# SwiGLU's first product by seven block products for eight in half of its chunks (one core of a Trainium2 chip)

## The chip, the cores and the metric

The kernel runs on one core of one Trainium2 chip. The metric is the device time of one execution in microseconds (us); three runs of the kernel before gave a median of 2055.57 us. Engines are named as in the profile: PE is TensorE (matmuls), PEld its weight loads, DVE is VectorE, ACT is ScalarE, POOL is GpSimd, SP is SyncE, which issues the loads.

## What is computed

One layer of a hybrid decoder on 256 tokens of width 2048 in float32: a mixer of three branches, a cross-attention, and the part that the change touches, a gated feed-forward of hidden width 5632:

```python
def swiglu(h, w13, w2):
    a, b = jnp.split(h @ w13, 2, axis=-1)
    return (jax.nn.silu(a.astype(jnp.float32)) * b.astype(jnp.float32)).astype(h.dtype) @ w2
...
        x = x + swiglu(rmsnorm(x, norm_ffn[i]), ffn_w13[i], ffn_w2[i])
    return rmsnorm(x, norm_final)
```

## The kernel before

**Blocks, chunks, halves.** Every product with a weight matrix is made in blocks of 512 output columns. A block's weights come as chunks of 512 rows (a tile `raw`, 128 x 4 x 512, 1 MB, loaded through SP's queue); a chunk is worked off in two halves of two 128-row tiles. The 256 tokens are two tiles of 128, so a block's result is 2 x 512 columns in PSUM, a tile `mm` of two banks; two such tiles exist, and four more banks of PSUM (`tp`) for everything else.

**Three products for one.** To keep float32's accuracy each operand is split in a high part, which TensorE's fp32r takes exactly, and the low rest. For a half chunk ScalarE makes the high part `wh` with one cast of 128x1024 (L161) and VectorE the low part `wl` by one subtraction of 128x1024 (L162). Then come, for two row tiles and two token tiles, three matmuls of 512 columns: high by high (L178), high by low (L179), low by high (L180): 12 for a half chunk. Activations are transposed and split the same way and kept (an `Act` with `hi` and `lo`).

**What sets the order.** The program is a list of halves and calls that is written out in order (`emit_half`); a half's split is emitted up to `LA = 3` halves ahead of its products, `wh` and `wl` have four buffers each and `raw` five. Evictions, transposes and the like are tasks that move one step after each half (`pump`). A scheduler then orders each engine's instructions by a simulated time; each engine works through its own list in order.

**SwiGLU.** The first product has 11 pairs of blocks: block i gives a, block 11 + i gives b, each of four chunks, 16 halves and 192 matmuls of 512 columns a pair. ScalarE makes silu of a, times the tokens' norm (L913), VectorE multiplies by b, times the norm again (L921); the result is transposed on TensorE (L264, two groups of four) and split (L268, L269) as `hT[i]`. The activations `x2T` carry the norm's gain but not the norm itself, which is multiplied in behind the product. After six pairs the second product (`w_2`) of those six chunks is added to the residual (L932), after the other five the rest.

## Time and profile before

| | |
|---|---|
| time, median of 3 runs | 2055.57 us (2055.42 to 2056.17) |
| span of the profiled execution (its time isn't listed apart from the span) | 2054.3 us |
| TensorE busy | 2042.2 us, 99% |
| VectorE busy | 1194.7 us, 58% |
| ScalarE busy | 959.8 us, 47% |
| matmuls of 128x512 in one pair of blocks | 192 |
| one pair of blocks | 44.45 us |

A row gives start and length in us, engine, line, operation, output and inputs (names without buffer numbers), and in brackets how long the engine had been idle and who released it. A matmul's row is longer than the distance to the next one, since matmuls overlap. A wait is put down to what came last.

### The profile page before, as it was taken

The page shows a single profiled execution, that of the slowest core. Times are in us where ns is not written, and L with a number is a line of the kernel's source. Part 1 is how long each engine was busy: PE and PEld are TensorE (multiplying, and loading weights), DVE is VectorE, ACT ScalarE, POOL GpSimd, SP SyncE. Part 2 cuts the span into 40 slices and gives each one's busy share as a digit, 9 for nine tenths or more (in the row PEclk, how much of TensorE's full clock was granted, in tenths as well). Part 3 has the DMA queues.
Part 4 walks back from the last instruction along what each step waited for, and adds up shares of the span by engine and source line. Part 5 has one row for each costly group of instructions (what it writes and reads, how often), then busy time and mean ns, then how long its engine had stood idle before and what let it go on. Part 6 is the DMA issues. An engine that isn't in the chain of part 4 may idle for free.

```text
span 2054.3 us, 23424 instructions
## 1 busy us (share of the span) xinstructions
PE 2042.2 (99%) x9369; PEld 1689.4 (82%) x9369; DVE 1194.7 (58%) x1505; ACT 959.8 (47%) x1190; POOL 20.3 (1%) x32
## 2 busy tenths in 40 slices
PE   9999999999999999999999999999999999999998
PEld 6888888888888888888888888888888888888886
DVE  6995699776654557444455555544455444455445
ACT  7444444558444455444445554444444334444443
POOL 0000000000000000000000000000000000000000
PEclk9999999999999999999999999999999999999999
DMA  9555444444555655655555444555555556555552
GB/s 374 185 188 202 174 175 174 166 164 163 186 212 196 220 200 215 227 203 185 200 186 182 151 149 158 184 185 188 196 189 184 189 200 207 195 192 185 185 199 88
DMA packets 57277, 390.33 MB, mean 190 GB/s; under 512 B 6480, under 2 KB 6736, under 8 KB 11984
## 3 DMA queue, kind: packets, MB, share of 16 engines
q1 hardware_dynamic: 54720, 380.44, 51.6%
q0 software_dynamic: 2304, 8.39, 1.1%
q8 instruction: 73, 1.20, 0.2%
q14 instruction: 36, 0.29, 0.0%
q10 hardware_dynamic: 144, 0.01, 0.0%
HBM read 386.72 MB, written 2.10 MB: 189 GB/s over the span
## 4 chain that ended last, share of the span: by engine, by line
PE 99%; DMA 0%; issue 0%; DVE 0%; SPq 0%; ACTq 0%; ACT 0%; POOLq 0%; POOL 0%
PE mm L178 31%; PE mm L179 31%; PE mm L180 31%; PE tp L264 1%; PE tp L178 1%; PE tp L179 1%; PE tp L180 1%; PE tp L283 0%; PE tp L832 0%; PE tp L831 0%; PE tp L830 0%; DMA raw<-in_w_in 0%; PE tp L622 0%; PE tp L558 0%; PE tp L620 0%
## 5 line engine op out<-in xcount | busy, mean ns | idle before, releaser
L162 DVE TENSOR_TENSOR wl<-raw,wh 128x1024 fp32r<-128x1024 f32 (+1 forms) x705 | 860.8, 1222 | 780.8 <-ACT wh L161 780.3
L161 ACT CAST wh<-raw 128x1024 fp32r<-128x1024 f32 (+1 forms) x705 | 740.8, 1052 | 956.2 <-PE mm L180 909.8
L178 PE MATMUL mm<-wh,s 128*128 128x512 f32 x2752 | 1078.4, 392 | 1.6 <-ACT wh L161 1.6
L179 PE MATMUL mm<-wl,s 128*128 128x512 f32 x2752 | 1075.3, 391 | 1.2 <-DVE wl L162 1.2
L180 PE MATMUL mm<-wh,s 128*128 128x512 f32 x2752 | 1073.7, 390 | 0.0
L178 PEld LDWEIGHTS mm<-wh,s 128*128 128x128 f32 x2752 | 516.8, 188 | 109.4 <-ACT wh L161 3.3
L180 PEld LDWEIGHTS mm<-wh,s 128*128 128x128 f32 x2752 | 516.7, 188 | 107.8
L179 PEld LDWEIGHTS mm<-wl,s 128*128 128x128 f32 x2752 | 517.0, 188 | 106.9 <-DVE wl L162 2.4
L433 DVE SCALAR_TENSOR_TENSOR s<-s,prm_t,s 128x227 f32<-128x227 f32 (+29 forms) x240 | 98.2, 464 | 0.0
L264 PE MATMUL tp<-cst_t,s 128*128 128x128 f32 x280 | 42.7, 272 | 0.0
L264 PEld LDWEIGHTS tp<-cst_t,s 128*128 128x128 f32 x280 | 34.5, 140 | 7.9
L269 DVE TENSOR_TENSOR s<-tp,s 128x512 fp32r<-128x512 f32 x46 | 31.1, 682 | 0.0
L251 ACT ACTIVATE s<-tp,prm_t 128x256 fp32r<-128x256 f32 x40 | 18.6, 472 | 19.1 <-DVE s L252 16.8
L268 ACT CAST s<-tp 128x512 fp32r<-128x512 f32 x46 | 26.4, 582 | 0.5 <-PE tp L264 0.5
L178 PE MATMUL tp<-wh,s 128*128 128x512 f32 x64 | 24.9, 389 | 0.0
L179 PE MATMUL tp<-wl,s 128*128 128x512 f32 x64 | 24.9, 389 | 0.0
L180 PE MATMUL tp<-wh,s 128*128 128x512 f32 x64 | 24.9, 389 | 0.0
L252 DVE SCALAR_TENSOR_TENSOR s<-tp,prm_t,s 128x256 fp32r<-128x256 f32 x40 | 19.0, 480 | 9.1 <-ACT s L251 9.1
L913 ACT ACTIVATE s<-mm,rs 128x512 f32<-128x512 f32 x22 | 13.9, 686 | 16.7 <-PE mm L180 16.7
L694 ACT ACTIVATE s<-mm,rsx 128x512 f32<-128x512 f32 x24 | 15.2, 685 | 12.5 <-PE mm L180 12.4
L296 ACT ACTIVATE s<-s 128x512 f32<-128x512 f32 x32 | 19.9, 624 | 1.4 <-DVE s L758 1.4
L921 DVE SCALAR_TENSOR_TENSOR s<-mm,rs,s 128x512 f32<-128x512 f32 x22 | 15.5, 747 | 4.6 <-PE mm L180 4.6
(172 smaller groups left out, 682.2 us busy)
## 6 DMA issues: line engine op xcount, KB each, us to landing
raw<-in_w SPq DMA_DIRECT2D x132, 1024.0 KB, 4.8
raw<-in_w_in SPq DMA_DIRECT2D x117, 1024.0 KB, 4.8
raw<-in_w_kv SPq DMA_DIRECT2D x32, 1024.0 KB, 4.8
raw<-in_w_br SPq DMA_DIRECT2D x24, 1024.0 KB, 4.8
raw<-in_w_out SPq DMA_DIRECT2D x16, 1024.0 KB, 4.8
raw<-in_w_q SPq DMA_DIRECT2D x16, 1024.0 KB, 4.9
raw<-in_w_o SPq DMA_DIRECT2D x16, 1024.0 KB, 4.8
raw<-in_w_in SPq DMA_DIRECT2D x5, 512.0 KB, 9.3
```

The source lines that it names most:

```text
L161: sc.copy(hi[:, sl, :], rv[:, sl, :])
L162: ve.tensor_tensor(out=lo[:, sl, :], in0=rv[:, sl, :], in1=hi[:, sl, :].bitcast(F32), op=ALU.subtract)
L178: nc.tensor.matmul(ps[t], ah, hi[:, k, :], start=j["start"] and k == 0, stop=False)
L179: nc.tensor.matmul(ps[t], ah, lo[:, k, :], start=False, stop=False)
L180: nc.tensor.matmul(ps[t], al, hi[:, k, :], start=False, stop=stop and k == 1)
L251: sc.activation(a.hi[:, k, :], src, AF.Identity, scale=g)
L252: ve.scalar_tensor_tensor(out=a.lo[:, k, :], in0=src, scalar=g, in1=a.hi[:, k, :].bitcast(F32), op0=ALU.mult, op1=ALU.subtract)
L264: nc.tensor.transpose(tp[:, k, t * P:(t + 1) * P], src(2 * pr + k, t), ident)
L268: sc.copy(a.hi[:, sl, :], tp)
L269: ve.tensor_tensor(out=a.lo[:, sl, :], in0=tp, in1=a.hi[:, sl, :].bitcast(F32), op=ALU.subtract)
L296: sc.activation(junk[:, t, :], tl[:, t, :], AF.Square, accum_out=dst[:, t:t + 1])
L433: ve.scalar_tensor_tensor(out=o[:, s:], in0=uT[:, k, :T - s], scalar=pc("cw", c * CW + CW - 1 - s), in1=o[:, s:], op0=ALU.mult, op1=ALU.add)
```

## The change

In ten of the eleven pairs (all but the first) two of the four chunks (`SC = (0, 1)`) are taken for both blocks at once. The activation chunk is seen as 2 x 2 blocks (token half by row half), the two weight chunks as 2 x 2 blocks (row half by block): a product of 2 x 2 blocks, by seven block products where eight would be the plain way. `quad_jobs` makes the seven units p1 to p7, each of six matmuls; three use the weights as they are (p1, p2, p3), four use differences of weight blocks, made in place in `raw` (L312) and split like the rest. On the activations' side the sums are made once, in `normalised` (`shi`, `slo`); it also multiplies the norm into the activations, so that silu and the product with the gate need it no more. p1, p5, p6 and p7 gather in four `tp` banks over both chunks, p2 and p4 go straight into the first block's `mm`, p3 into the second's. `leave` combines the four banks into two tiles (L372 on ScalarE, L373 to L376 on VectorE); the other two chunks follow by halves as before, and `done` adds the combined tile to each block (L384) before silu and the product. While the two chunks run, tasks that need a `tp` bank are held back (`lock`).

With it come: the first pair taken chunk by chunk in turn (`pair_n`), so that `normalised` can begin; three groups of the second product instead of two (after pairs 3, 7 and 10, counted from 0); `LA = 4`; six buffers for `wh` and `wl`, four for `raw`, 27 for `s4`, which now also holds cross-attention's score tiles (`SX`).

```diff
-LA = 3
+LA = 4
...
-    rawp = ctx.enter_context(tc.tile_pool(name="rawp", bufs=5))
-    hlp = ctx.enter_context(tc.tile_pool(name="hlp", bufs=4))
-    s4 = ctx.enter_context(tc.tile_pool(name="s4", bufs=28))
+    rawp = ctx.enter_context(tc.tile_pool(name="rawp", bufs=4))
+    hlp = ctx.enter_context(tc.tile_pool(name="hlp", bufs=6))
+    s4 = ctx.enter_context(tc.tile_pool(name="s4", bufs=27))
...
+    def lhs(a, kind, q, k):
+
+        if kind == "n":
+            t, k0 = q
+            return tuple(x[:, k0 + k, t * P:(t + 1) * P] for x in (a.hi, a.lo))
+        return tuple(x[:, q, k * P:(k + 1) * P] for x in (a.shi, a.slo))
...
+    def emit_unit(i):
+        while state["made"] < min(i + 1 + min(LA, 1 + i), len(units)):
+            emit_group()
+        u = units[i]
+        need(u["act"])
+        for pr in u["prods"]:
+            if pr[1] not in pr[0]:
+                u["alloc"](pr[0])
+        products(u, u.get("ts"))
+        if not u["keep"]:
+            u["hi"] = u["lo"] = None
...
+    def quad_jobs(pp, ps0, ps1, w0, w1, a):
+
+
+        c0, c1 = add_chunk(w0), add_chunk(w1)
+
+        def unit(ps, key, k0, t, kind):
+            u = add_unit([(ps, key, k0, t, kind)], a)
+            u["alloc"] = alloc_tp1 if ps is pp else alloc_mm
+            return u
+
+        def alloc_tp1(ps):
+            for k in (1, 5, 6, 7):
+                ps[k] = TP()
+
+        p1 = unit(pp, 1, 0, 0, "n")
+        p5 = unit(pp, 5, 0, 0, "s")
+        p2 = unit(ps0, 0, 2, 0, "n")
+        p6 = unit(pp, 6, 0, 1, "s")
+        p3 = unit(ps1, 0, 0, 3, "s")
+        p7 = unit(pp, 7, 0, 2, "s")
+        p4 = unit(ps0, 1, 2, 1, "n")
+
+        def b(ci, j):
+            return raw(ci)[:, 2 * j:2 * j + 2, :]
+
+        def sub(o, x, y):
+            ve.tensor_tensor(out=o, in0=x, in1=y, op=ALU.subtract)
+
+        def both(t, make, u, v, src):
+
+            parts_of(u)
+            parts_of(v)
+            make()
+            hi_of(v, src)
+            hi_of(u, t)
+            lo_of(v, src)
+            lo_of(u, t)
+
+        def g0():
+            raw(c1)
+            parts_of(p1)
+            hi_of(p1, b(c0, 0))
+            lo_of(p1, b(c0, 0))
+
+        def g1():
+            t = b(c0, 0)
+            both(t, lambda: sub(t, b(c1, 0), t), p5, p2, b(c0, 1))
+
+        def g2():
+            t = b(c0, 0)
+            both(t, lambda: sub(t, b(c1, 1), t), p6, p3, b(c1, 1))
+
+        def g3():
+            t3, t4 = b(c1, 0), b(c0, 0)
+            parts_of(p7)
+            parts_of(p4)
+            sub(t3, b(c1, 1), t3)
+            sub(t4, b(c0, 1), t4)
+            hi_of(p7, t3)
+            hi_of(p4, t4)
+            lo_of(p7, t3)
+            lo_of(p4, t4)
+            raws.pop(c0)
+            raws.pop(c1)
+
+        groups.extend([([p1], g0), ([p5, p2], g1), ([p6, p3], g2), ([p7, p4], g3)])
+        return [p1, p5, p2, p6, p3, p7, p4]
...
+    def pair(W0, W1, acts, modes, evac0, evac1):
+
+
+        ps0, ps1, pp = {}, {}, {}
+        xs = []
+        us = []
+        sset = [c for c in range(len(acts)) if modes[c] == "S"]
+        nset = [c for c in range(len(acts)) if modes[c] == "N"]
+
+        def enter():
+            for c in sset:
+                need(acts[c])
+            settle()
+            lock[0] = True
+
+        def leave():
+            x0, x1 = S4([P, 2, 512]), S4([P, 2, 512])
+            a1, u3, u2, v = x0[:, 0, :], x0[:, 1, :], x1[:, 0, :], x1[:, 1, :]
+            sc.copy(a1, pp[1])
+            ve.tensor_tensor(out=u2, in0=pp[6], in1=a1, op=ALU.add)
+            ve.tensor_tensor(out=u3, in0=pp[7], in1=u2, op=ALU.add)
+            ve.tensor_tensor(out=u2, in0=pp[5], in1=u2, op=ALU.add)
+            ve.tensor_tensor(out=v, in0=pp[5], in1=u3, op=ALU.add)
+            pp.clear()
+            xs.extend([x0, x1])
+            lock[0] = False
+
+        def done(n, ps, evac):
+            def f():
+                x = xs[n]
+                ve.tensor_tensor(out=x, in0=ps["m"], in1=x, op=ALU.add)
+                xs[n] = None
+                evac(x)
+            return f
+
+        call(enter)
+        for c in sset:
+            us += quad_jobs(pp, ps0, ps1, W0[c], W1[c], acts[c])
+        call(leave)
+        us += half_jobs(ps0, [W0[c] for c in nset], [acts[c] for c in nset])
+        call(done(0, ps0, evac0))
+        us += half_jobs(ps1, [W1[c] for c in nset], [acts[c] for c in nset])
+        call(done(1, ps1, evac1))
+        close(us)
...
+    def pair_n(W0, W1, acts, evac0, evac1, after):
+
+        ps0, ps1 = {}, {}
+        us = []
+        for c in range(len(acts)):
+            us += half_jobs(ps0, [W0[c]], [acts[c]])
+            us += half_jobs(ps1, [W1[c]], [acts[c]])
+            call(lambda c=c: after(c))
+        call(lambda: evac0(ps0["m"]))
+        call(lambda: evac1(ps1["m"]))
+        close(us)
...
-        return sm.tile([P, 2, 256], dt, tag="sx", name=nm("sx"), bufs=3)
+        return S4([P, 2, 256], dt)
...
-    def ev_a(i):
+    def ev_a(i, rs=None):
         def f(ps):
+            if rs is None:
+                sc.activation(ps, ps, AF.Silu)
+                ff[i] = ps
+                return
             drain(rst["ffn"])
             s = S4([P, 2, 512])
             for t in range(2):
-                sc.activation(s[:, t, :], ps[:, t, :], AF.Silu, scale=rs2[:, t:t + 1])
+                sc.activation(s[:, t, :], ps[:, t, :], AF.Silu, scale=rs[:, t:t + 1])
             ff[i] = s
         return f
 
-    def ev_b(i):
+    def ev_b(i, rs=None):
         def f(ps):
             s = ff.pop(i)
-            for t in range(2):
-                ve.scalar_tensor_tensor(out=s[:, t, :], in0=ps[:, t, :], scalar=rs2[:, t:t + 1], in1=s[:, t, :],
-                                        op0=ALU.mult, op1=ALU.mult)
+            if rs is None:
+                ve.tensor_tensor(out=s, in0=ps, in1=s, op=ALU.mult)
+            else:
+                for t in range(2):
+                    ve.scalar_tensor_tensor(out=s[:, t, :], in0=ps[:, t, :], scalar=rs[:, t:t + 1],
+                                            in1=s[:, t, :], op0=ALU.mult, op1=ALU.mult)
             hT[i].task = spawn(transposed(hT[i], blk(s), None))
         return f
+
+    SC = (0, 1)
...
+    def normalised(src, dst, rs, free):
+
+        while len(free) < 1:
+            yield 2
+        dg = S4([P, 2, P])
+        on = S4([P, P])
+        ve.memset(on, 1.0)
+        for t in range(2):
+            ve.tensor_scalar(out=dg[:, t, :], in0=ident, scalar1=rs[:, t:t + 1], scalar2=None, op0=ALU.mult)
+        yield
+        tp = TP()
+        for t in range(2):
+            nc.tensor.matmul(tp[:, t * P:(t + 1) * P], on, dg[:, t, :], start=True, stop=True)
+        yield 1
+        rb = S4([P, 256])
+        sc.copy(rb, tp[:, 0:256])
+        dg = on = tp = None
+        yield 2
+        for c in range(4):
+            while len(free) < c + 1:
+                yield 2
+            q = S4([P, 4, 256])
+            ve.tensor_tensor(out=q, in0=src[c].hi.bitcast(F32), in1=src[c].lo.bitcast(F32), op=ALU.add)
+            ve.tensor_tensor(out=q, in0=q, in1=rb[:, None, :].broadcast_to([P, 4, 256]), op=ALU.mult)
+            src[c].hi = src[c].lo = None
+            yield 2
+            a = dst[c]
+            a.hi, a.lo = S4([P, 4, 256], F32R), S4([P, 4, 256], F32R)
+            sc.copy(a.hi, q)
+            ve.tensor_tensor(out=a.lo, in0=q, in1=a.hi.bitcast(F32), op=ALU.subtract)
+            yield 2
+            if c in SC:
+                f = S4([P, 4, 256])
+                fv = f.rearrange("p i (k c) -> p i k c", k=2)
+                a11, a12, a21, a22 = (q[:, 2 * k:2 * k + 2, t * P:(t + 1) * P] for t in range(2) for k in range(2))
+                for o, x, y, op in ((0, a21, a22, ALU.add), (1, fv[:, 0], a11, ALU.subtract),
+                                    (2, a11, a21, ALU.subtract), (3, a12, fv[:, 1], ALU.subtract)):
+                    ve.tensor_tensor(out=fv[:, o], in0=x, in1=y, op=op)
+                yield 2
+                a.shi, a.slo = S4([P, 4, 256], F32R), S4([P, 4, 256], F32R)
+                sc.copy(a.shi, f)
+                ve.tensor_tensor(out=a.slo, in0=f, in1=a.shi.bitcast(F32), op=ALU.subtract)
+                f = fv = None
+            q = None
+            yield 2
 
...
+    x2n = [Act() for _ in range(4)]
+    free = []
+
+    def after(c):
+        free.append(c)
+        if c == 0:
+            drain(rst["ffn"])
+            t = spawn(normalised(x2T, x2n, rs2, free))
+            for a in x2n:
+                a.task = t
+
     def ffn_pairs(r):
         for i in r:
-            block(w_13, i, x2T, ev_a(i))
-            block(w_13, 11 + i, x2T, ev_b(i))
+            w0, w1 = ([w_13[n, c] for c in range(4)] for n in (i, 11 + i))
+            if i == 0:
+                pair_n(w0, w1, x2T, ev_a(i, rs2), ev_b(i, rs2), after)
+            else:
...
-    ffn_pairs(range(0, 6))
+    for lo in (0, 4):
+        ffn_pairs(range(lo, lo + 4))
+        for nb in range(4):
+            block(w_2[:, lo:lo + 4], nb, hT[lo:lo + 4], ev_w2(nb))
+    ffn_pairs(range(8, 11))
```

**VectorE in a pair.** Of the kernel before, around the end of a pair: the splits of the last halves (`wl`), the product with the gate (L921), the next pair's splits with the two evictions of transposes (L269).

```order
L162 TENSOR_TENSOR wl_1742_10507<-raw_1740_10504,wh_1741_10506 128x1024
L162 TENSOR_TENSOR wl_1744_10523<-raw_1740_10504,wh_1743_10522 128x1024
L162 TENSOR_TENSOR wl_1747_10541<-raw_1745_10538,wh_1746_10540 128x1024
L921 SCALAR_TENSOR_TENSOR s4_1726_10416<-mm_1729_10423,rs2_98,s4_1726_10416 128x512 x2
L162 TENSOR_TENSOR wl_1749_10559<-raw_1745_10538,wh_1748_10558 128x1024
L162 TENSOR_TENSOR wl_1756_10585<-raw_1754_10582,wh_1755_10584 128x1024
L162 TENSOR_TENSOR wl_1758_10603<-raw_1754_10582,wh_1757_10602 128x1024
L269 TENSOR_TENSOR s4_1752_10576<-tp_1753_10577,s4_1751_10575 128x512
```

Of the kernel after, the end of the first two chunks of the third pair: p3's split, then the splits and subtractions of p6, p7 and p4 in the second chunk, with the combining rows and one eviction (L472) between them, and the split of the first half behind (`raw_1817`).

```order
L184 TENSOR_TENSOR wl_1812_10726<-raw_1801_10689,wh_1811_10725 128x1024
L312 TENSOR_TENSOR raw_1800_10687<-raw_1801_10689,raw_1800_10687 128x1024
L184 TENSOR_TENSOR wl_1810_10724<-raw_1800_10687,wh_1809_10723 128x1024
L184 TENSOR_TENSOR wl_1814_10745<-raw_1801_10689,wh_1813_10744 128x1024
L312 TENSOR_TENSOR raw_1800_10687<-raw_1800_10687 128x1024
L373 TENSOR_TENSOR s4_1828_10811<-tp_1793_10656,s4_1827_10810 128x512
L472 TENSOR_TENSOR s4_1833_10836<-tp_1834_10837,s4_1832_10835 128x512
L374 TENSOR_TENSOR s4_1827_10810<-tp_1794_10657,s4_1828_10811 128x512
L184 TENSOR_TENSOR wl_1816_10747<-raw_1800_10687,wh_1815_10746 128x1024
L375 TENSOR_TENSOR s4_1828_10811<-tp_1792_10655,s4_1828_10811 128x512
L376 TENSOR_TENSOR s4_1828_10811<-tp_1792_10655,s4_1827_10810 128x512
L184 TENSOR_TENSOR wl_1819_10769<-raw_1817_10766,wh_1818_10768 128x1024
```

The same engine that had one row per 12 matmuls now has p6's subtraction directly ahead of p6's split, and two combining rows and the eviction ahead of p4's.

**ScalarE there.** Of the kernel after, the casts that belong to these splits: p3, then the copy of p1's bank, p6, p7, the eviction of transposes, and p4.

```order
L181 CAST wh_1811_10725<-raw_1801_10689 128x1024
L372 COPY s4_1827_10810<-tp_1791_10654 128x512
L181 CAST wh_1809_10723<-raw_1800_10687 128x1024
L181 CAST wh_1813_10744<-raw_1801_10689 128x1024
L471 CAST s4_1832_10835<-tp_1834_10837 128x512
L181 CAST wh_1815_10746<-raw_1800_10687 128x1024
```

p6's cast reads what the subtraction on VectorE has just written, and stands behind the copy that waits for p1.

**VectorE in the second pair.** Of the kernel after, in the first chunk of the first pair that works in the new way: the rows of `normalised` (L1159 sum of parts, L1160 norm, L1166 low part) stand between the splits of the weights.

```order
L184 TENSOR_TENSOR wl_1717_10290<-raw_1703_10223,wh_1716_10289 128x1024
L184 TENSOR_TENSOR wl_1732_10340<-raw_1704_10225,wh_1731_10339 128x1024
L1160 TENSOR_TENSOR s4_1720_10310<-s4_1720_10310,s4_1683_10118 128x1024
L312 TENSOR_TENSOR raw_1703_10223<-raw_1703_10223 128x1024
L1166 TENSOR_TENSOR s4_1723_10319<-s4_1720_10310,s4_1722_10318 128x1024
L1159 TENSOR_TENSOR s4_1724_10322<-s4_1658_9982,s4_1659_9983 128x1024
L184 TENSOR_TENSOR wl_1734_10342<-raw_1703_10223,wh_1733_10341 128x1024
L184 TENSOR_TENSOR wl_1739_10367<-raw_1736_10362,wh_1738_10366 128x1024
L1160 TENSOR_TENSOR s4_1724_10322<-s4_1724_10322,s4_1683_10118 128x1024
L184 TENSOR_TENSOR wl_1743_10379<-raw_1736_10362,wh_1742_10378 128x1024
L312 TENSOR_TENSOR raw_1736_10362<-raw_1737_10364,raw_1736_10362 128x1024
L1166 TENSOR_TENSOR s4_1726_10326<-s4_1724_10322,s4_1725_10325 128x1024
```

Before, no row of this kind stood in the pairs.

## Rows read from the trace of the kernel before

**Rows 1.** The page: span, and busy time of each engine.
```profile
span 2054.3 us, 23424 instructions
PE 2042.2 (99%) x9369; PEld 1689.4 (82%) x9369; DVE 1194.7 (58%) x1505; ACT 959.8 (47%) x1190; POOL 20.3 (1%) x32
```

**Rows 2.** The page: the chain that ended last, shares by engine.
```profile
PE 99%; DMA 0%; issue 0%; DVE 0%; SPq 0%; ACTq 0%; ACT 0%; POOLq 0%; POOL 0%
```

**Rows 3.** Windows: stretch, length, busy us, clock, DMA share; a pair and the end.
```profile
1360.99:1405.44 44.45, 44.45 (x201) 36.73 (x200) 22.12 (x20) 18.91 (x21) 0.00 (x0) 1.00 0.52 187
...
2042.00:2054.00 12.00, 4.17 (x19) 3.13 (x17) 6.20 (x13) 5.32 (x12) 1.12 (x2) 0.85 0.46 175
```

**Rows 4.** Waits: engine, line, releaser, total us, times, longest us.
```profile
ACT wh L161 <- PE mm L180: 909.8, 574, 6.1
DVE wl L162 <- ACT wh L161: 780.3, 557, 6.5
```

**Rows 5.** Timeline around the end of one half chunk in a pair, all engines.
```profile
1379.33 1.23 DVE L162 TENSOR_TENSOR wl<-raw,wh 128x1024 fp32r<-128x1024 f32 x1 [1.50 <-ACT wh L161]
...
1380.08 0.39 PE L178 MATMUL mm<-wh,s 128*128 128x512 f32 x1
...
1380.31 0.39 PE L179 MATMUL mm<-wl,s 128*128 128x512 f32 x1
...
1380.53 0.39 PE L180 MATMUL mm<-wh,s 128*128 128x512 f32 x1
...
1380.76 0.39 PE L178 MATMUL mm<-wh,s 128*128 128x512 f32 x1
...
1380.96 1.05 ACT L161 CAST wh<-raw 128x1024 fp32r<-128x1024 f32 x1 [1.67 <-PE mm L180]
...
1382.05 1.23 DVE L162 TENSOR_TENSOR wl<-raw,wh 128x1024 fp32r<-128x1024 f32 x1 [1.49 <-ACT wh L161]
```

**Rows 6.** Timeline of TensorE around a group of four transposes.
```profile
1369.16 0.39 PE L180 MATMUL mm<-wh,s 128*128 128x512 f32 x1
1369.39 0.60 PE L264 MATMUL tp<-cst_t,s 128*128 128x128 f32 x4
1369.74 0.48 PE L178 MATMUL mm<-wh,s 128*128 128x512 f32 x1
1370.06 0.40 PE L179 MATMUL mm<-wl,s 128*128 128x512 f32 x1
```

**Rows 7.** VectorE by line and form: count, busy us, mean ns, idle before.
```profile
L701 DVE TENSOR_TENSOR s<-mm,s 128x1024 f32<-128x1024 f32 x12 | 14.7, 1223 | 3.6 <-PE mm L180 3.6
...
L705 DVE TENSOR_TENSOR s<-s,s 128x1024 f32<-128x1024 f32 x8 | 9.8, 1219 | 0.0
```

**Rows 8.** Timelines of VectorE, five stretches: rows that follow each other closely.
```profile
121.56 0.68 DVE L511 TENSOR_TENSOR s<-mm,rope 128x512 f32<-128x512 f32 x1
122.16 0.41 DVE L512 TENSOR_TENSOR s<-mm,rope 128x256 f32<-128x256 f32 x1
122.49 0.41 DVE L514 TENSOR_TENSOR s<-mm,rope 128x256 f32<-128x256 f32 x1
...
609.93 1.23 DVE L701 TENSOR_TENSOR s<-mm,s 128x1024 f32<-128x1024 f32 x1 [0.41 <-PE mm L180]
611.07 1.22 DVE L162 TENSOR_TENSOR wl<-raw,wh 128x1024 fp32r<-128x1024 f32 x1
612.20 1.22 DVE L705 TENSOR_TENSOR s<-s,s 128x1024 f32<-128x1024 f32 x1
...
1247.16 0.16 DVE L859 RECIPROCAL tn<-tn 128x2 f32<-128x2 f32 x1
1247.36 0.62 DVE L861 TENSOR_SCALAR sx<-sx,tn 128x256 f32<-128x256 f32 x2
...
1342.74 2.36 DVE L162 TENSOR_TENSOR wl<-raw,wh 128x1024 fp32r<-128x1024 f32 x2 [3.94 <-ACT wh L161]
...
1405.44 1.41 DVE L921 SCALAR_TENSOR_TENSOR s<-mm,rs,s 128x512 f32<-128x512 f32 x2 [0.41 <-PE mm L180]
1406.77 1.22 DVE L162 TENSOR_TENSOR wl<-raw,wh 128x1024 fp32r<-128x1024 f32 x1
```

**Rows 9.** ScalarE by line and form, as rows 7: the casts of the weights.
```profile
L161 ACT CAST wh<-raw 128x1024 fp32r<-128x1024 f32 x703 | 739.5, 1053 | 953.2 <-PE mm L180 909.8 <-PE tp L180 13.5 <-DVE s L433 10.0
```

**Rows 10.** The page: loads of weights, count, KB each, us from issue to landing.
```profile
raw<-in_w SPq DMA_DIRECT2D x132, 1024.0 KB, 4.8
```

228 lines of the change are left out of this document (137 added, 91 removed).

## The prediction

> **What bounds the kernel now.** I read the page's busy line first, then the chain, then single stretches. TensorE is busy for 2042.2 of 2054.3 us and 99% of the chain that ended last is its matmuls [rows 1, 2]. In one block pair of SwiGLU's first product (from the product of one pair, L921, to that of the next) TensorE is busy for all 44.45 us at the full clock, 1.00, while VectorE works 22.12 us and ScalarE 18.91 us [rows 3]. So what TensorE no longer does is gained there, as long as nobody makes it wait. Nobody does now: the long waits are the other way round, ScalarE's casts for TensorE (909.8 us, to get a buffer back) and VectorE's subtractions for those casts (780.3 us) [rows 4].
>
> A row calls a matmul 0.39 us long, but one starts every 0.227 us (1380.08, 1380.31, 1380.53, 1380.76) [rows 5]. A half chunk is 12 matmuls, 2.72 us, and VectorE's splits come at just that distance [rows 5]. Four transposes cost 0.44 us: L180 to the second matmul behind them is 0.90 us (1369.16 to 1370.06), less two steps of 0.227 [rows 6]. A pair is then 16 x 2.72 + 2 x 0.44 = 44.4 us, as measured.
>
> **What is removed.** A chunk of both blocks was 4 half chunks of 12 matmuls, 48; it is now seven units of 6, 42. Two chunks in each of ten pairs: 120 matmuls fewer, 120 x 0.227 = **27.2 us**. By TensorE alone a pair would take 14 x 1.36 + 8 x 2.72 + 0.88 = 41.7 us. I call its first 14 units (p1, p5, p2, p6, p3, p7, p4, and the same with a dash) the S stage, ideally 19.04 us plus 0.88 of the previous pair's transposes, and the eight half chunks behind them N1 to N8.
>
> **What is added, and to whom.** Every unit still wants a high part (ScalarE, 1.05 us [rows 9]) and a low part (VectorE), though it now feeds only 1.36 us of matmuls and not 2.72. Each quad adds four subtractions of 128x1024 on VectorE; each pair adds four of 128x512 to combine the products, and two additions of 128x1024 and one product of that size in place of two 128x512 ones. The forms are in the trace: 128x1024 takes 1.22 us whether an operand is in PSUM (L701) or all are in SBUF (L705) [rows 7]; where VectorE has a queue, the next starts 1.13 to 1.14 us later (609.93, 611.07, 612.20; two splits in 2.36 us), 0.61 behind a 128x512, 0.33 behind a 128x256 [rows 8]. A pair then asks VectorE for 33 x 1.14 + 6 x 0.61 = 41.3 us, against TensorE's 41.7. That would just fit if the work were spread evenly, but it isn't: an S stage wants 22 of the long ones in 19 us.
>
> How far ahead can VectorE be when an S stage starts? Six high and low parts exist, so a unit can be split only when the sixth unit before it has left TensorE. Call the end of N8 zero. The buffer of p3 is that of N7, which is free at -2.72 + 0.20 (the cast starts 0.20 us after the next unit's first matmul, 1380.76 to 1380.96 [rows 5]); with the cast and 0.04 us to VectorE [rows 5] p3's low part starts at -1.43 and VectorE is free at -0.29. What stands behind it up to the low part of N1, by the order built from the new kernel, is: low part of p6; a subtraction; the second block's addition; p7; the product with the gate; p4; p1'; p2'; two subtractions; p5'; p3'; a subtraction; p6'; p7'; a subtraction; two combining steps with an eviction of the previous pair between them; p4'; two combining steps; N1. That is 18 x 1.14 + 5 x 0.61 = 23.57 us. To it comes one wait: p6' is cast only when the subtraction ahead of its low part is done, and nothing stands between the two on VectorE, 1.10 us (the cast and its hand-over). The subtraction that overwrites what p6 has just read waits for that row's end, 0.10, and N1's matmul for the last row's end, 0.12 (a dependent row starts 0.04 us behind the end, 1247.16 + 0.16 to 1247.36 [rows 8]). N1's low part is there at -0.29 + 23.57 + 1.10 + 0.22 = 24.6. TensorE wanted it at 19.04 + 0.88 + 0.23 = 20.15. **It waits 4.45 us per pair**, first ahead of p6', most of it ahead of p4' and N1. The saving was 2.72 us. The low parts up to p5' are in time (p5' at 12.3, wanted at 12.5), and N1 to N8 give VectorE time to be stopped by the buffers again, so that each pair begins alike. This holds for seven pairs (2, 3, 5, 6, 7, 9, 10, counted from 0): 31.2 us.
>
> Pairs 4 and 8 come behind blocks of the second product: no product with the gate (1.14) and no eviction (0.61) stand in the queue, N1's low part is there at 22.85, but there are no transposes either and TensorE wants it at 19.27: 3.6 us each, 7.2.
>
> Pair 1 comes behind pair 0, in which the activations are normalised and added up for the new products. Its p3 starts at -1.43 as well, but behind it stand 24 long rows instead of 18 (the rest of the normalising) and the two 0.66 us steps of pair 0's product (1405.44 to 1406.77 for two [rows 8]): 8.2 us more, 12.6 us.
>
> Two small matmuls for the normalising cost 0.2 us. Loads stay what they were, one chunk of 1 MB for each of the same chunks. With four raw buffers for five the tightest is N5's: its buffer is free when p4' is split, at 22.3, a load lands in 4.8 us [rows 10], at 27.1, and TensorE comes to N5 at 35: nothing, and a late start by up to 4.8 us if this cover were gone. Four more additions for the third group of second-product blocks lie in stretches where VectorE is half idle: nothing. The score tiles of cross-attention that now share a pool with everything else I set at 0, between 0 and 4 us: a few waits of one long VectorE row (1.22 us [rows 7]); TensorE's order there is nearly the old one.
>
> **The sum.** -27.2 + 31.2 + 7.2 + 12.6 + 0.2 = +24.0 us on a span of 2054.3, 2078.3. The median of the three runs is 1.3 us above that span, so **2079.5 us**, 1.2% slower.
>
> Bounds: without the wait at p6' (were ScalarE's cast in time) each pair waits 1.1 us less, 2068.5. If no VectorE row overlapped its neighbour, 1.25 us each instead of 1.14 (0.70 for 0.61), a pair waits 18 x 0.11 + 5 x 0.09 = 2.4 us more, ten pairs and pair 1's six more rows 25 us, 2104. The dense rows are of the same forms, so I stay near their value.
>
> **Rivals.**
> - *VectorE is far enough ahead.* Its 41.3 us per pair fit into TensorE's 41.7. If it ran so far ahead that the S stage found all its parts made, ten pairs would give 27.2 us, less some 8 us in pair 1, whose extra rows are real: 2036, faster. It decides at a mean wait of 2.7 us per pair. Against it speak the six buffers, which hold it at p3 until N7 is through, and the evictions in the middle of its queue. 0.10.
> - *The two nearly cancel*: the waits are as in the walk without p6' and some rows are shorter still; within 4 us of before. 0.06.
> - *VectorE's rows don't overlap once every row waits for ScalarE or for the row ahead*, the upper bound: 2104. For it speaks the dependent row; against it the two splits in 2.36 us, each of which had its own cast to wait for [rows 8]. 0.10.
> - *The clock falls in the waits.* The clock is 0.85 in the last 12 us, where TensorE works 4.17 us [rows 3]; nowhere else in the pairs is there idle time to learn from. Were half of an S stage run at 1.2 GHz, each pair would lose another 9.5 us: 2170. The waits are pieces of 1 to 2 us between matmuls, which is why I give it 0.04.
> - My forecast, 2064 to 2092: 0.70.
>
> The Trainium skill (VectorE: DVE Perf Modes, Terms) has each DVE operation followed by a drain that keeps the next from issuing until the pipe is empty. By that rule the third rival would be right and the sum would be about +49 us; the trace disagrees, 1.14 us from start to start for rows of 1.22.
>
> **How the numbers follow.** What a measurement of this kernel can tell from no change is about 0.2%, 4 us. Faster 0.10, same 0.06, slower 0.84. The range takes in the forecast's bounds and most of the third rival: 2062 to 2098; left out are the first two, the clock and the far end, 2 in 10.
>
> **What would show it.** In the page after: 120 fewer matmuls of 128x512; TensorE no longer 99% busy but some 51 us idle, nearly all ahead of the matmuls that read a low part, with VectorE's split as releaser; in a window over one pair about 46.2 us, with VectorE near 41 us busy by starts, dense from p6 to N1, and stopped by casts in the N stage. Pair 1 longest, 4 and 8 shortest. Wrong would be: pairs of 42 us (the first rival), TensorE waiting for loads or for ScalarE, VectorE rows 1.25 us apart, or a granted clock under 0.95 in the pairs.

## The result, and the profile after

The changed kernel takes 2072.87 us (median of four runs, 2071.63 to 2074.52) against 2055.53 for the kernel before: 1.0084 times, 95% interval 1.007 to 1.0098. It is slower by 17.3 us, where 24 were predicted.

The page after, answering [rows 1, 2]: span, busy time of each engine, the chain that ended last by engine and by line.

```profile
span 2069.5 us, 23555 instructions
PE 2032.5 (98%) x9253; PEld 1668.3 (81%) x9253; DVE 1414.0 (68%) x1724; ACT 1025.4 (50%) x1257; POOL 20.3 (1%) x32
PE 85%; DVE 10%; issue 3%; ACT 1%; DMA 0%; SPq 0%; ACTq 0%; POOLq 0%; POOL 0%; DVEq 0%
PE mm L257 27%; PE mm L258 27%; PE mm L256 26%; DVE wl L184 5%; DVE raw L312 3%; PE tp L467 1%; ACT wh L181 1%; PE tp L258 0%; PE tp L257 0%; PE tp L256 0%; PE tp L487 0%; DVE s L1127 0%; DVE s L384 0%; PE tp L1035 0%; PE tp L1034 0%
```

The chain was 99% TensorE. Now 10% of it is VectorE: the splits (L184) and the subtractions of weight blocks (L312). The waits (engine, line, releaser: us in total, times, longest) say the same, answering [rows 4]:

```profile
PE mm L257 <- DVE wl L184: 20.2, 22, 1.3
...
ACT wh L181 <- PE mm L258: 762.0, 497, 6.2
ACT wh L181 <- DVE raw L312: 74.5, 31, 3.8
...
DVE wl L184 <- ACT wh L181: 567.3, 426, 6.5
```

The windows from p1's first matmul of one pair to that of the next, answering [rows 3]: pairs 2 and 5, pair 1, pair 4 (behind blocks of the second product). Columns: length, busy us of PE, PEld, DVE, ACT, POOL, clock, DMA share, GB/s.

```profile
1413.01:1458.42 45.41, 43.09 (x189) 34.31 (x188) 41.69 (x40) 24.84 (x26) 0.00 (x0) 1.00 0.49 185
1635.65:1681.03 45.38, 43.04 (x190) 34.29 (x189) 41.70 (x40) 24.85 (x26) 0.00 (x0) 1.00 0.50 186
1360.97:1413.01 52.04, 45.06 (x189) 34.13 (x188) 48.38 (x47) 27.38 (x29) 0.00 (x0) 1.00 0.44 162
1591.80:1635.65 43.85, 41.69 (x181) 33.64 (x180) 39.54 (x37) 23.89 (x24) 0.00 (x0) 1.00 0.51 192
```

A pair has gone from 44.45 to 45.4 us, with VectorE at 41.7 (41.3 in the prediction) and the clock at 1.00. VectorE around the S stage of pair 2, in order (p1's first matmul, the end of N8, is at 1413.01):

```profile
1409.12 1.22 DVE L184 TENSOR_TENSOR wl<-raw,wh 128x1024 fp32r<-128x1024 f32 x1
1411.62 1.22 DVE L184 TENSOR_TENSOR wl<-raw,wh 128x1024 fp32r<-128x1024 f32 x1 [1.28 <-ACT wh L181]
1412.88 1.22 DVE L312 TENSOR_TENSOR raw<-raw 128x1024 f32<-128x1024 f32 x1
1414.02 1.22 DVE L384 TENSOR_TENSOR s<-mm,s 128x1024 f32<-128x1024 f32 x1
...
1425.52 1.22 DVE L312 TENSOR_TENSOR raw<-raw,raw 128x1024 f32<-128x1024 f32 x1
1427.91 2.36 DVE L184 TENSOR_TENSOR wl<-raw,wh 128x1024 fp32r<-128x1024 f32 x2 [1.17 <-ACT wh L181]
1430.19 1.22 DVE L312 TENSOR_TENSOR raw<-raw 128x1024 f32<-128x1024 f32 x1
1431.32 0.68 DVE L373 TENSOR_TENSOR s<-tp,s 128x512 f32<-128x512 f32 x1
1431.92 0.68 DVE L472 TENSOR_TENSOR s<-tp,s 128x512 fp32r<-128x512 f32 x1
1432.52 0.68 DVE L374 TENSOR_TENSOR s<-tp,s 128x512 f32<-128x512 f32 x1
1433.12 1.21 DVE L184 TENSOR_TENSOR wl<-raw,wh 128x1024 fp32r<-128x1024 f32 x1
1434.25 0.68 DVE L375 TENSOR_TENSOR s<-tp,s 128x512 f32<-128x512 f32 x1
1434.85 0.68 DVE L376 TENSOR_TENSOR s<-tp,s 128x512 f32<-128x512 f32 x1
1435.45 4.62 DVE L184 TENSOR_TENSOR wl<-raw,wh 128x1024 fp32r<-128x1024 f32 x4
```

p3's low part is the row at 1409.12, p6's that at 1411.62; the row at 1433.12 is p4', and N1's ends 1.22 us behind 1435.45. The only stop from 1411.62 on is the 1.17 us at 1427.91, p6' waiting for the cast of what the subtraction ahead of it has just written. TensorE waits for the two rows of p4' and N1, and before them its transposes wait:

```profile
1432.06 0.66 PE L467 MATMUL tp<-cst_t,s 128*128 128x128 f32 x4 [0.30 <-DVE s L373]
1432.60 0.50 PE L256 MATMUL mm<-wh,s 128*128 128x512 f32 x1
1434.39 0.50 PE L257 MATMUL mm<-wl,s 128*128 128x512 f32 x1 [1.29 <-DVE wl L184]
...
1435.65 0.39 PE L256 MATMUL mm<-wh,s 128*128 128x512 f32 x1
1436.72 0.50 PE L257 MATMUL mm<-wl,s 128*128 128x512 f32 x1 [0.68 <-DVE wl L184]
```

Here the printed wait is too small. From start to start it is 1434.39 - 1432.60 = 1.79, less a step of 0.227, 1.56 us lost, where the row says 1.29: the row ahead, drawn 0.5 us long, covers part of the gap. In the same way N1 loses 1436.72 - 1435.65 - 0.227 = 0.84 us. The four transposes lose 0.46 (the matmul ahead of them starts at 1431.37); the profile puts that down to the first combining step (L373), which reads a `tp` bank, and the prediction has no such wait. So the page, too, shows only 37.0 us of TensorE not busy (12.1 before). The ruler for what is lost is the run without subtractions, below.

### The profile page after: what moved, and what is told of

The parts are those of the page before. It is cut to its first block, busy times and chain, and to the rows that moved or that the text cites. A ratio compares the mean times of both kernels' runs of the same rounds, so it can differ in the third digit from the quotient of the medians.

```text
span 2069.5 us, 23555 instructions
## 1 busy us (share of the span) xinstructions
PE 2032.5 (98%) x9253; PEld 1668.3 (81%) x9253; DVE 1414.0 (68%) x1724; ACT 1025.4 (50%) x1257; POOL 20.3 (1%) x32
## 4 chain that ended last, share of the span: by engine, by line
PE 85%; DVE 10%; issue 3%; ACT 1%; DMA 0%; SPq 0%; ACTq 0%; POOLq 0%; POOL 0%; DVEq 0%
PE mm L257 27%; PE mm L258 27%; PE mm L256 26%; DVE wl L184 5%; DVE raw L312 3%; PE tp L467 1%; ACT wh L181 1%; PE tp L258 0%; PE tp L257 0%; PE tp L256 0%; PE tp L487 0%; DVE s L1127 0%; DVE s L384 0%; PE tp L1035 0%; PE tp L1034 0%
## 5 line engine op out<-in xcount | busy, mean ns | idle before, releaser
L184 DVE TENSOR_TENSOR wl<-raw,wh 128x1024 fp32r<-128x1024 f32 x763 | 922.7, 1221 | 568.5 <-ACT wh L181 567.3
L181 ACT CAST wh<-raw 128x1024 fp32r<-128x1024 f32 x763 | 794.5, 1052 | 894.0 <-PE mm L258 762.0
L257 PE MATMUL mm<-wl,s 128*128 128x512 f32 x2584 | 1012.3, 392 | 20.2 <-DVE wl L184 20.2
L256 PE MATMUL mm<-wh,s 128*128 128x512 f32 x2584 | 1014.3, 393 | 2.1 <-ACT wh L181 1.7
L258 PE MATMUL mm<-wh,s 128*128 128x512 f32 x2584 | 1008.7, 391 | 0.0
L256 PEld LDWEIGHTS mm<-wh,s 128*128 128x128 f32 x2584 | 486.2, 188 | 104.9 <-ACT wh L181 2.8
L258 PEld LDWEIGHTS mm<-wh,s 128*128 128x128 f32 x2584 | 486.0, 188 | 100.9 <-issue 0.3
L256 PE MATMUL tp<-wh,s 128*128 128x512 f32 x192 | 75.5, 396 | 2.2 <-ACT wh L181 1.9
L257 PE MATMUL tp<-wl,s 128*128 128x512 f32 x192 | 75.6, 393 | 0.8 <-DVE wl L184 0.8
L258 PE MATMUL tp<-wh,s 128*128 128x512 f32 x192 | 74.8, 390 | 0.0
L312 DVE TENSOR_TENSOR raw<-raw 128x1024 f32<-128x1024 f32 x40 | 48.8, 1221 | 0.6
L312 DVE TENSOR_TENSOR raw<-raw,raw 128x1024 f32<-128x1024 f32 x40 | 48.8, 1220 | 0.6
L256 PEld LDWEIGHTS tp<-wh,s 128*128 128x128 f32 x192 | 36.0, 188 | 13.8 <-ACT wh L181 6.7
L258 PEld LDWEIGHTS tp<-wh,s 128*128 128x128 f32 x192 | 36.1, 188 | 6.9
L472 DVE TENSOR_TENSOR s<-tp,s 128x512 fp32r<-128x512 f32 x46 | 30.6, 680 | 0.0
```

The source lines that it names most:

```text
L181: sc.copy(u["hi"], src)
L184: ve.tensor_tensor(out=u["lo"], in0=src, in1=u["hi"].bitcast(F32), op=ALU.subtract)
L256: nc.tensor.matmul(o, ah, u["hi"][:, k, :], start=fl in u["start"] and k == 0, stop=False)
L257: nc.tensor.matmul(o, ah, u["lo"][:, k, :], start=False, stop=False)
L258: nc.tensor.matmul(o, al, u["hi"][:, k, :], start=False, stop=fl in u["stop"] and k == 1)
L312: ve.tensor_tensor(out=o, in0=x, in1=y, op=ALU.subtract)
```

## Experiments

**What TensorE alone would need, and whether VectorE's rows are the cause.** The four subtractions of a quad are left out:

```diff
         def sub(o, x, y):
-            ve.tensor_tensor(out=o, in0=x, in1=y, op=ALU.subtract)
+            pass
```

> Left out: the four subtractions of weight blocks in every quad (eight VectorE rows of 128x1024 in each of ten pairs); the units that should use differences use a plain block. Everything else, the combining too, stays. My theory (VectorE's queue at the S stage is the wait): five of those rows stand between p3 and N1, 5.7 us, more than the 3.5 us of wait, so the wait is gone: 2054.3 less 27.2 plus at most 3 in pair 1, 2029 to 2034 with what lies around the span. Rival (casts that wait for buffers, hand-overs between engines, the banks): most of the wait stays, 2055 or more.

Measured: 2029.88 us, 0.9874 (0.9859 to 0.9889). A steady pair in it, by windows:

```profile
1402.93:1444.75 41.82, 41.82 (x190) 34.52 (x188) 33.14 (x31) 25.58 (x26) 0.00 (x0) 1.00 0.54 201
```

TensorE is busy for the whole pair, 41.82 us (41.7 by the prediction's steps). Against this run, the changed kernel's pairs are longer by 9.9 (pair 1), 3.1 (4 and 8), 4.25 (6) and 3.6 (all others, with the stretches that hold them): together 41.8 us, and the spans differ by 41.9. All of the loss is in those ten places. (Pair 6 is longer than its neighbours because the clock fell in it; see the end.) This edit takes out the subtractions' rows and with them the casts' waits for those rows, so it does not tell the two apart; the runs below do that in part.

**The edits that were costed at nothing.** All pairs by plain halves, nothing normalised, the other edits kept:

```diff
-            t = spawn(normalised(x2T, x2n, rs2, free))
-            for a in x2n:
-                a.task = t
...
-                pair(w0, w1, x2n, ["S" if c in SC else "N" for c in range(4)], ev_a(i), ev_b(i))
+                block(w_13, i, x2T, ev_a(i, rs2))
+                block(w_13, 11 + i, x2T, ev_b(i, rs2))
```

> All eleven pairs by plain halves on the activations without the norm, as in the kernel before; nothing is normalised and no quad is made. The other edits of the change stay: four halves of lookahead, six buffers for the parts, four for the raw chunks, the score tiles in the common pool, three groups of the second product, the first pair chunk by chunk. My theory (the whole loss lies in the quads and the normalising): within 2 us of the kernel before, 2053 to 2058. Rival (the buffers, the lookahead or the score tiles cost something): 2060 or more, with the waits ahead of the feed-forward part or at loads.

Measured: 2056.48, 1.0003 (0.9994 to 1.0013). Lookahead, buffers, score tiles and the third group cost nothing that can be measured.

**Two rows more.** In each quad one row of 128x1024 behind `sub(t3, ...)`:

```diff
             sub(t3, b(c1, 1), t3)
+            ve.tensor_tensor(out=t3, in0=t3, in1=t3, op=ALU.max)
```

> One VectorE row of 128x1024 more in every quad (the maximum of a difference with itself, which changes nothing), two per pair. Nothing is left out. My theory: both stand in the queue between p3 and N1, so each pair waits two rows of 1.14 us longer, with hand-overs 2.3 to 2.6: 2072.9 plus 23 to 26, 2096 to 2099. Rival (TensorE is late for another reason than VectorE's queue, so the rows fall into gaps): under 8 us more.

Measured: 2091.24, 1.0176 (1.0159 to 1.0193): 18.4 more, between the two expectations. A steady pair is 46.84 us, 1.43 longer instead of 2.3. VectorE at the start of an S stage, the first added row at 1411.46 (lines below it are one higher):

```profile
1411.46 1.22 DVE L343 TENSOR_TENSOR raw<-raw 128x1024 f32<-128x1024 f32 x1
...
1415.21 1.22 DVE L184 TENSOR_TENSOR wl<-raw,wh 128x1024 fp32r<-128x1024 f32 x1 [0.27 <-ACT wh L181]
1416.81 1.22 DVE L385 TENSOR_TENSOR s<-mm,s 128x1024 f32<-128x1024 f32 x1 [0.37 <-PE mm L258]
```

VectorE still stands still twice behind that row, until a buffer and the end of N8 come: the first row falls into the 1.28 us that it stood still anyway. A row costs TensorE time only from there on, and the second one does: 1.14 us. The other 0.3 come from the order: the second block's addition (L385) now stands ahead of p4's subtraction, and starts 0.2 us behind N8 instead of 1.01. Ten pairs with 1.43 us make 14.3 of the 18.4; in the profiled execution the clock also falls in six places (the mean over the run is 0.994, against 0.998 in the changed kernel).

**Later combining.** The first of the four combining steps is pinned behind the splits that stand ahead of it in the program:

```diff
-            ve.tensor_tensor(out=u2, in0=pp[6], in1=a1, op=ALU.add)
+            tc.keep_in_program_order(ve.tensor_tensor(out=u2, in0=pp[6], in1=a1, op=ALU.add))
```

> One edit: the first combining step is pinned behind the splits that stand ahead of it in the program, so that in VectorE's order the four combining steps and the eviction of transposes come behind the splits of N1 to N4 and no longer ahead of p4' and N1. Nothing is left out. My theory (N1's low part is late by the length of VectorE's queue): five steps of 0.61 us leave the queue, N1's low part comes 3.05 us earlier, against a wait of about 3.5 us in the changed kernel; what is left is some 0.5 us per pair at p6' and N1 and pair 1's extra. About 2.9 us less in seven pairs, 2.4 in two, 3 in pair 1: 2072.9 less 28, some 2045 (2040 to 2052), faster than before. TensorE's waits for the low part fall from 49 us to under 20. Rival (the waits come from something else than the rows in that queue: the cast at p6', the buffers, the locked banks): under 8 us less, 2065 or more; or the transposes wait for the banks instead and the time stays.

Measured: 2076.08, 1.0102 (1.0087 to 1.0117). My expectation was wrong by 31 us: the five short rows did leave the queue, and nothing was won. VectorE in pair 2:

```profile
1417.49 1.22 DVE L312 TENSOR_TENSOR raw<-raw 128x1024 f32<-128x1024 f32 x1
1419.90 3.50 DVE L184 TENSOR_TENSOR wl<-raw,wh 128x1024 fp32r<-128x1024 f32 x3 [1.19 <-ACT wh L181]
...
1427.97 1.22 DVE L312 TENSOR_TENSOR raw<-raw,raw 128x1024 f32<-128x1024 f32 x1
1430.36 2.36 DVE L184 TENSOR_TENSOR wl<-raw,wh 128x1024 fp32r<-128x1024 f32 x2 [1.17 <-ACT wh L181]
1432.64 1.22 DVE L312 TENSOR_TENSOR raw<-raw 128x1024 f32<-128x1024 f32 x1
1435.02 5.77 DVE L184 TENSOR_TENSOR wl<-raw,wh 128x1024 fp32r<-128x1024 f32 x5 [1.17 <-ACT wh L181]
```

Three stops instead of one (so in pairs 2, 6, 7 and 10; the other six have two). A subtraction, the cast of its result on ScalarE and the low part of that are a chain; with nothing between, VectorE stands still 1.17 to 1.19 us. In the changed kernel the three short rows between p4's subtraction and p4' had covered that. In pair 2 two long rows are in the way as well: p6's low part and p4's subtraction now stand behind the second block's addition, which starts 0.2 us behind N8 and not 1.01. Short rows -3.05, two more stops +2.36, two long rows +2.28, the earlier start -0.8: N1's low part should come 0.8 us later than in the changed kernel, and it is there 24.6 us behind p1's first matmul, against 23.7. Taking rows out of a queue is worth something only where no such chain opens in their place. There is a second loss here, of the clock, told at the end; the profiled execution is the slowest of the four (2080.58).

**The order inside a quad.** If that is so, the same number of rows in a better order should be enough: the plain block's low part between a subtraction and the low part of its difference.

```diff
-            lo_of(v, src)
+            lo_of(v, src, True)
             lo_of(u, t)
...
-            lo_of(p7, t3)
+            lo_of(p7, t3, True)
             lo_of(p4, t4)
```

(`True` pins the row behind the one that stands before it on VectorE in the program; the line of `lo_of` that does this isn't shown.)

> One edit: inside a quad VectorE's order is the program's. The low part of the plain block (p2, p3) stands between the subtraction and the low part of its difference, and p7's low part stands behind p4's subtraction. The combining steps stay where the changed kernel has them. Nothing is left out. Theory after the run with the later combining: two things make N1's low part late, the rows in VectorE's queue and the chain subtraction, cast, low part, in which VectorE stands still for 1.1 to 1.2 us per quad unless another row lies between; so each of the two rows moved fills such a gap. From the addition of the second block (0.2 us behind N8) to N1 stand 17 rows of 1.14 and one of 0.61, 20.1 us; N1 is wanted at 20.15. About 0.5 us of wait left per pair, and pair 1's 8: 2054.3 less 27.2 plus 5 plus 8, with 1.3 around the span 2041 (2037 to 2048). Rival (only the number of rows counts, and their number is unchanged up to p4'): as the changed kernel, 2070 or more.

Measured: 2045.17, 0.9948 (0.9933 to 0.9963), above the expected 2041 but within its bounds. 27.7 us come back, and no row is removed. VectorE at the end of the S stage of pair 2 (p1's first matmul is at 1411.93):

```profile
1423.73 1.23 DVE L312 TENSOR_TENSOR raw<-raw,raw 128x1024 f32<-128x1024 f32 x1
1424.87 2.48 DVE L184 TENSOR_TENSOR wl<-raw,wh 128x1024 fp32r<-128x1024 f32 x2
1427.39 1.22 DVE L312 TENSOR_TENSOR raw<-raw 128x1024 f32<-128x1024 f32 x1
1428.53 1.22 DVE L184 TENSOR_TENSOR wl<-raw,wh 128x1024 fp32r<-128x1024 f32 x1
1429.67 0.68 DVE L373 TENSOR_TENSOR s<-tp,s 128x512 f32<-128x512 f32 x1
1430.27 2.35 DVE L184 TENSOR_TENSOR wl<-raw,wh 128x1024 fp32r<-128x1024 f32 x2
1432.54 0.68 DVE L374 TENSOR_TENSOR s<-tp,s 128x512 f32<-128x512 f32 x1
```

Two things have changed here and not one. Three low parts are pinned in each quad; in pair 2 this moves p2', p3' and p7' in the second quad, each behind a subtraction, and no stop is left. But the scheduler has also put four of the five short rows behind N1 (L374 is the first of them); only L373 is still ahead of it. So the combining steps do not stay where the changed kernel has them. N1's low part is there 1432.62 - 1411.93 = 20.69 us behind p1's first matmul, against 23.66. Of these 3.0 us the stop gives 1.17 and the four short rows 4 x 0.60 = 2.4; 0.6 are lost again, about half of them because p4's subtraction now stands behind the second block's addition. What the order of the long rows is worth by itself this run doesn't show. Both edits together:

> Both edits: the order of the program inside a quad, and the combining steps behind the splits of N1 to N4. Nothing is left out. By the theory of two causes the 0.61 us row that still stands ahead of N1 is gone too, and the waits are gone but for pair 1: 2035 to 2046, no slower than the order inside the quads alone. Rival (the later combining costs something of its own, the banks come late for the transposes, or the clock falls): 2055 or more.

Measured: 2044.86, 0.9942 (0.9926 to 0.9959). The later combining neither costs nor gains once the order inside the quads is mended; it had one short row left to move. Against the later combining alone, where all five short rows are behind N1 too, this run differs by the order inside the quads only: 2076.08 to 2044.86, 31.2 us. Of these the falls of the clock (told at the end) are an estimated 8 at most, five dips of 1.6 us in the profiled execution of the one and none in that of the other. Pair 2 of this run by windows:

```profile
1411.66:1454.41 42.75, 42.10 (x190) 34.41 (x189) 41.33 (x39) 24.62 (x26) 0.00 (x0) 1.00 0.50 197
```

No subtraction is followed by a stop in any S stage of this run. VectorE is as busy as before (41.33 of 42.75), but a pair is only 0.9 us longer than TensorE's 41.82.

**One chunk, and three.** `SC = (0,)`, all else as in the changed kernel:

> One of the four chunks by seven products instead of two; the other three by halves. 60 matmuls fewer than the kernel before, 13.6 us. In VectorE's order seven long rows stand from p6's low part to N1's, some 8 us from 1.4 us ahead of the end of N8, and TensorE wants N1 9.8 us behind it; the combining steps stand apart between the splits of N1 to N6. My theory (what a pair waits is what VectorE's queue is longer than the S stage): no wait in steady pairs, 0 to 4 us in pair 1: 2042 to 2047, faster than before and than the changed kernel. Rival (each quad costs its own wait, half of the changed kernel's 41 us): 2062 to 2064.

Measured: 2045.06, 0.9949 (0.9934 to 0.9964). By windows a pair takes 43.14 us, all of it busy:

```profile
1406.24:1449.38 43.14, 43.14 (x196) 35.70 (x194) 34.28 (x33) 22.45 (x23) 0.00 (x0) 1.00 0.54 195
```

Half the quads cost a steady pair no wait at all (pair 1 is 1.75 us longer): the loss is not a price per quad, which fits with a loss by what the S stage asks of VectorE beyond its own length. `SC = (0, 1, 2)`, in the order of the quads, with the later combining and a plain pair 1:

> As the version with the order inside the quads, the later combining and a plain pair 1, but three of the four chunks by seven products. Nothing is left out. TensorE would need 21 x 1.36 + 4 x 2.72 + 0.9 = 40.4 us per pair; VectorE has 40 long rows and 6 short ones, 40 x 1.14 + 6 x 0.61 = 49.3. My theory (VectorE's rows set the pair as soon as they are more than TensorE's time): pairs of about 49 us, nine of them 6.7 us longer, up to 10 us given back behind the blocks of the second product: 2088 to 2102. Rival (only the order of the rows matters, not their sum): 2030 or less.

Measured: 2101.3 in a single run. Pairs 5 and 2, by windows:

```profile
1634.24:1685.26 51.02, 43.59 (x184) 32.70 (x182) 50.28 (x47) 27.25 (x29) 0.00 (x0) 1.00 0.46 166
1406.26:1449.82 43.56, 41.53 (x184) 33.15 (x182) 43.16 (x40) 25.48 (x27) 0.00 (x0) 1.00 0.51 193
```

In pair 5 VectorE is busy for 50.28 of 51.02 us: its rows are the bound, and no order of the same rows could give much back. Pairs 6 and 9 are like it (50.5 and 50.1 us). Pairs 2, 4 and 8, the first ones behind plain halves or behind blocks of the second product, take 43.1 to 43.6.

**Pair 1.** By plain halves on the normalised activations, quads from pair 2 on; pair 1's silu then goes to a tile in SBUF, as before the change:

```diff
+        if not sset:
+            close(half_jobs(ps0, W0, acts))
+            call(lambda: evac0(ps0["m"]))
+            close(half_jobs(ps1, W1, acts))
+            call(lambda: evac1(ps1["m"]))
+            return
...
-                sc.activation(ps, ps, AF.Silu)
-                ff[i] = ps
+                s = ps if i > 1 else S4([P, 2, 512])
+                sc.activation(s, ps, AF.Silu)
+                ff[i] = s
...
-                pair(w0, w1, x2n, ["S" if c in SC else "N" for c in range(4)], ev_a(i), ev_b(i))
+                pair(w0, w1, x2n, ["S" if c in SC and i > 1 else "N" for c in range(4)], ev_a(i), ev_b(i))
```

> The second pair (pair 1) by plain halves on the normalised activations, quads from the third pair on. Nothing is left out. 12 matmuls more, 2.7 us. Theory: pair 1 waits 10.2 us in the changed kernel because the rows that make the sums stand in its S stage; they now fall beside plain halves, where VectorE has time, so pair 1 waits nothing, and pair 2 waits as the others: 2072.9 plus 2.7 less 10, 2065 to 2067. Rival (the first pair that works in the new way always pays, whichever it is): 2074 to 2077.

Measured: 2065.38, 1.0044 (1.0029 to 1.0059): 7.5 us come back. The normalising rows cost only where they stand in an S stage.

**Five buffers for the parts.**

```diff
-    hlp = ctx.enter_context(tc.tile_pool(name="hlp", bufs=6))
+    hlp = ctx.enter_context(tc.tile_pool(name="hlp", bufs=5))
```

> The changed kernel with five buffers for the high and the low parts instead of six. Nothing is left out. My theory (the buffers set how far ahead of the S stage VectorE can be): p6's part takes the buffer of N8, not of N7, so its low part comes behind N8 and stands in the queue as one more row, 1.14 us, less what VectorE then no longer stands still ahead of N8's end, about 0.8: 0.3 to 1.4 us more per pair, 3 to 14 more in all, 2076 to 2087. Rival (six were more than is used): within 2 us of 2072.9.

Measured: 2099.94, 1.0213 (1.0199 to 1.0227), 27 more instead of 3 to 14: the sign was right, the size not. A steady pair is 48.1 us, 2.7 longer. The rows explain it: the addition of the second block (L384) now comes 0.2 us behind N8 and not 1.01, which gains 0.8; but p6's low part and p4's subtraction, which the changed kernel had done ahead of it, now stand behind it, 1.14 each, and a second stop on a cast opens ahead of p4, 1.19. -0.8 + 2.28 + 1.19 = 2.7. I had counted one row and not the chain.

**The subtractions on GpSimd.**

```diff
         def sub(o, x, y):
-            ve.tensor_tensor(out=o, in0=x, in1=y, op=ALU.subtract)
+            nc.gpsimd.tensor_tensor(out=o, in0=x, in1=y, op=ALU.subtract)
```

> The eight subtractions of weight blocks per pair are made by GpSimd instead of VectorE; everything else as in the changed kernel. Nothing is left out. GpSimd is busy for 20 us of the kernel and no row here has its time for 128x1024. My theory (VectorE's queue is what waits): if a row takes GpSimd under 1.6 us and VectorE keeps its 1.14 us, the waits go but for the chain on p6 and p4: 2034 to 2050. If GpSimd takes over 2.3 us a row (four in a row in one block, with a cast and a split between them, in 9.5 us of a quad), it is the new bound and the time is above the changed kernel's: over 2075. I hold the second for likelier, 0.6 to 0.4.

Measured: 2141.36, 1.0416 (1.0401 to 1.043), the second case. The mean granted clock of this run is 0.984 (0.998 in the changed kernel), so not all of the 68 us are GpSimd's rows; what each is worth isn't separated. GpSimd's rows (min, median, max in ns), and a VectorE split that ran beside one:

```profile
L312 POOL TENSOR_TENSOR raw<-raw,raw x40: 2393/3303/3464, 1350.8 to 2031.8; 128x1024 f32<-128x1024 f32 x40
L312 POOL TENSOR_TENSOR raw<-raw x40: 2357/2843/3317, 1354.3 to 2037.5; 128x1024 f32<-128x1024 f32 x40
...
1422.55 2.51 DVE L184 TENSOR_TENSOR wl<-raw,wh 128x1024 fp32r<-128x1024 f32 x1
```

**The best version.** The order inside the quads, the later combining and the plain pair 1:

> The order inside the quads, the combining behind N1 to N4, and pair 1 by plain halves on the normalised activations. Nothing is left out. In the run with the first two edits pair 1 lasted 49.0 us; plain halves give 44.4, and the first matmul of the quads no longer comes 1.7 us late. If the three edits work on different places, 2044.9 less 6, 2037 to 2041. Rival (pair 2 then carries what pair 1 carried): 2044 or more.

Measured: 2038.27 (2037.46 to 2038.56), 0.9913 (0.9899 to 0.9926), as expected. It beats the kernel before by 17.6 us and the changed kernel by 34.6.

## Why the prediction was right, and where it was off

- **The saving, 27.2 us**: 120 matmuls of 128x512 fewer (8448 rows of that form before, 8328 after), and without waits a pair takes 41.82 us against 44.45. Right.
- **The mechanism**, VectorE's queue through the S stage ending at N1: right. With the eight subtractions gone from it the waits are gone; one row more in its dense part costs that row and 0.3 us more.
- **The size in steady pairs, 4.45**: 3.6 measured. The step that failed is the start of the walk. I gave p3 the buffer of N7, by the program's order of the units. The scheduler splits p3 ahead of p6 (p3's block needs no subtraction), and buffers go round in that order: the cast for the row at 1409.12 starts at 1407.82, before p6's block is written (by the subtraction at 1407.98) and 0.25 us behind N7's first matmul. So p3 has the buffer of N6, and it is p6's low part that starts at 1411.62 - 1413.01 = -1.39, where I had p3's at -1.43. One long row less stands behind that point: 17 and not 18. N1's low part is there at 1436.67 - 1413.01 = 23.66; the walk said 24.6.
- **Pairs 4 and 8, 3.6; pair 1, 12.6**: 3.1 and 9.9. The same row is missing in each. In pair 4 N1's low part is there 1613.92 - 1591.80 = 22.1 us behind N8, where the walk said 22.85. In pair 1 the row explains some 0.9; its other 1.8 us I have not traced row by row. That its extra comes from the normalising is shown by the plain pair 1.
- **The wait at p6', 1.10**: 1.17 measured, one in each S stage. The term was right, but I took it for a detail of one row. The runs show that it belongs to every subtraction that nothing covers (two or three in an S stage with the later combining alone), and that the order in which nothing is left uncovered turns the sign of the change; that order also lets the short rows go behind N1.
- **The edits at nothing**: right, by the run without quads.
- **The sum**: the span is 2069.5 where the sum gives 2078.3, 8.8 less: waits of 41.8 for 51.0, and 0.4 more in small things. The median lies 3.4 us above the profiled span, where 1.3 was assumed, 2.1 more; the two errors go against each other and leave the difference of 6.6 between 2079.5 and 2072.9. The 2.1 are not the kernel's. Every run that lists both is 1.7 to 2.3 us longer than its span. The profiled execution of the changed kernel (2071.63) was the fastest of its four. That of the kernel before, 2054.3 and the usual 2.0, took an estimated 2056.3, which is above the median of its runs, and so 1.3 was too little.
- **The rivals**: VectorE far enough ahead became true only in another order of its rows. Rows that don't overlap: refuted, the dense rows start 1.13 to 1.14 us apart in the new stretch too (1431.32 - 1430.19 = 1.13). The clock stays 1.00 in nine of the ten pairs; in pair 6 it is 0.96, and that pair is 0.7 us longer than its neighbours. But the idle TensorE time was to be read off the page as some 51 us, and the page shows 25 more than before; that was the wrong place to look, since matmul rows cover part of a gap.

## What to carry to other kernels

When a change takes work from the bound engine and gives some to another, compare the two over the stage that got the work, not over the loop: 41.3 against 41.7 us per pair looked like a fit, and a stage of 19 us with 22 long rows did not fit. Then look for hand-overs to another engine and back between neighbouring rows (subtract, cast, subtract): each stops an in-order queue for the whole of the other engine's step unless an independent row lies between. Taking five short rows out of the queue won nothing here, because such stops opened in their place; with the same rows out and the long ones in an order without stops, 31 us were won, most of them by the order. For the size of a loss, use a run in which the suspected rows are left out as the ruler, and starts of matmuls, not the printed waits.
